# Rotary embedding on one core: three TensorE rows of eight instead of four, and the last tile stored as one transfer

## The chip, the cores and the metric

One core of a Trainium2 chip (trn2). The metric is device time in microseconds; smaller is better. A run's profile also gives its span, the time from the first to the last instruction of the core, which is 1.7 to 2.4 us shorter than the device time. The first three runs of the kernel before agree within 0.05 us (its profiled run took 163.37 us).

## The reference

`x` is 16 batches of 512 positions with 1024 float32 values, seen as 16 heads of 64. Each head is rotated by a per-position table:

```python
x1, x2 = x[..., :32], x[..., 32:]              # halves of each head
cos, sin = cos[None, :, None, :], sin[None, :, None, :]
rotated = concatenate([x1 * cos - x2 * sin, x1 * sin + x2 * cos], axis=-1)
```

So an output is `x * cos + swapped(x) * signed_sin`: two multiplies and an add per element, 33.6 MB in and 33.6 MB out.

## The kernel before

There are eight tiles of 128 partitions. A tile is 4 MiB: per partition eight rows (`k` = 0 to 7) of 1024 values. Loads and stores are all issued from SyncE (SP), in one queue; five tile buffers are allotted in SBUF, the core's working memory, so the loads of tiles 5 to 7 wait for the stores of tiles 0 to 2.

```python
PE_ROWS = (0, 2, 4, 6)       # rows whose sum is made by TensorE in PSUM
DVE_B = ((0,), (0, 4))       # rows whose sine product VectorE makes itself (even, odd tiles)
FIRST = (3, 8)               # tile 0 is loaded as rows 0-2 and rows 3-7
LAST_OUT = (4, 8)            # tile 7 is stored as rows 0-3 and rows 4-7
...
pe = ctx.enter_context(tc.tile_pool(name="pe", bufs=2, space=bass.MemoryType.PSUM))
pd = ctx.enter_context(tc.tile_pool(name="pd", bufs=1, space=bass.MemoryType.PSUM))
...
def add():
    r, ps, b = pending.pop(0)
    nc.vector.tensor_tensor(out=r, in0=ps, in1=b, op=ALU.add)

for t in range(NT):
    xt = tiles[t]
    for k in range(KK):
        r = xt[:, k * dim : (k + 1) * dim]
        own = k in DVE_B[t % 2]
        if not own:
            b = bp.tile([P, dim], FP32, name="b")
            ...
            nc.gpsimd.tensor_tensor(out=halves(b), in0=swapped(r, nh), in1=over_heads(sk), op=ALU.mult)
        if k in PE_ROWS:
            ps = pe.tile([P, dim], FP32, name="ps")
            nc.vector.tensor_tensor(out=pairs(ps), in0=pairs(r), in1=cos_b(k), op=ALU.mult)
            if own:
                nc.vector.tensor_tensor(out=halves(r), in0=halves(r), in1=swapped_signed(k), op=ALU.mult)
            for c in range(0, dim, BANK):
                ...
                nc.tensor.matmul(out=ps[:, c : c + BANK], lhsT=ident, rhs=rhs, start=False, stop=True, ...)
            nc.scalar.copy(out=r, in_=ps)
            while pending:
                add()
        else:
            while pending:
                add()
            ps = pd.tile([P, dim], FP32, name="pd")
            nc.vector.tensor_tensor(out=pairs(ps), in0=pairs(r), in1=cos_b(k), op=ALU.mult)
            pending.append((r, ps, b))
    while pending:
        add()
    if t < NT - 1:
        store(t)
    else:
        lo = 0
        for hi in LAST_OUT:
            store(t, lo, hi)
            lo = hi
    if t + 1 == NT - BUFS:
        for n in range(BUFS, NT):
            load(n)
```

(Cuts are marked with `...`; the code shown is otherwise as in the kernel.) A row costs VectorE one cosine multiply. A TensorE row then gets its sine product added in PSUM, the memory that takes TensorE's sums, by a matmul with the identity, and ScalarE copies the sum back over `x`. Any other row gets a VectorE add. GpSimd makes most sine products.

Of the kernel before, what the change touches and what calls it, by code (L numbers as in the profile page):

```python
# [14 lines left out]
B_BUFS = 6  # L15
BANK = 512

PE_ROWS = (0, 2, 4, 6)

DVE_B = ((0,), (0, 4))  # L20

FIRST = (3, 8)
LAST_OUT = (4, 8)

SIN_PARTS = (64,)
COS_PARTS = (64,)


@with_exitstack
def kernel(  # L30
# [13 lines left out]
    nc = tc.nc  # L44
# [12 lines left out]
    cos_v = cos.rearrange("(p k) j -> p (k j)", k=KK)  # L57
    sin_v = sin.rearrange("(p k) j -> p (k j)", k=KK)
# [18 lines left out]
    def store(t, lo=0, hi=KK):  # L77
        s = slice(lo * dim, hi * dim)
        nc.sync.dma_start(out=out_v[t][:, s], in_=tiles[t][:, s])

    load(0, 0, FIRST[0])
    sin_sb = bp.tile([P, dim], FP32, name="b")[:PB, : KK * half]
    cos_sb = bp.tile([P, dim], FP32, name="b")[:PB, : KK * half]
    for sb, v, parts in ((sin_sb, sin_v, SIN_PARTS), (cos_sb, cos_v, COS_PARTS)):
        lo = 0
        for hi in parts:
            nc.sync.dma_start(out=sb[lo:hi, :], in_=v[lo:hi, :])
            lo = hi
    for lo, hi in zip(FIRST, FIRST[1:]):
        load(0, lo, hi)  # L90
    for t in range(1, BUFS):
# [22 lines left out]
    nc.vector.tensor_copy(out=sns[:, :, 1, :], in_=sin_k)  # L114
    on_dve = sorted(set(DVE_B[0]) | set(DVE_B[1]))
    sns_t = tab[:, KK * half : KK * half + len(on_dve) * hd]
# [7 lines left out]
    def over_heads(s):  # L124
        return bass.AP(tensor=s.tensor, offset=s.offset, ap=[s.ap[0], [0, nh], [1, hd]])

    def swapped(r, n):
        return bass.AP(
            tensor=r.tensor, offset=r.offset + half, ap=[r.ap[0], [hd, n], [-half, 2], [1, half]]
        )  # L130
# [12 lines left out]
    def halves(r):  # L143
        return r.rearrange("p (h a j) -> p h a j", a=2, j=half)
# [7 lines left out]
# [7 lines that stand above are left out]
                sk = sns[:, k].rearrange("p a j -> p (a j)")  # L159
# [3 lines that stand above are left out]
# [3 lines left out]
                for c in range(0, dim, BANK):  # L166
                    rhs = swapped(r[:, c : c + BANK], BANK // hd) if own else b[:, c : c + BANK]
                    nc.tensor.matmul(  # L168
                        out=ps[:, c : c + BANK], lhsT=ident, rhs=rhs, start=False, stop=True, skip_group_check=True
# [14 lines left out]
# [5 lines that stand above are left out]
# [38 lines left out]
```

## Time and profile before

| | before |
|---|---|
| time, median of three runs | 163.11 us |
| span of the profiled run | 161.6 us |
| DMA queue, share of 16 engines' span | 97.5% |
| VectorE busy, last instruction ends | 128.9 us, 142.96 us |
| last store issued, landed | 143.03 us, 160.5 us |
| granted TensorE clock, mean (share of full speed) | 0.833 |

The first lines to read are the page's busy times, its slices (each digit is the busy share of a fortieth of the span, in tenths) and its table of DMA queues (packets, MB, share of the span of all 16 engines).

```profile
PE 81.8 (51%) x136; PEld 30.3 (19%) x136; DVE 128.9 (80%) x115; ACT 33.7 (21%) x33; POOL 121.0 (75%) x58
...
DVE  1059897999999989999999999999999999930000
...
PEclk9999996559975998799969965999689879995555
DMA  5999999999999999999999999999999999999992
...
q1 hardware_dynamic: 2752, 67.24, 97.5%
```

The DMA row has nines from the second slice to the last but one: the queue never runs out of work. VectorE stops four slices earlier. Its 80% looks high, but it has time to spare at the end.

The groups of the page that the change touches (busy time, mean ns of one instruction, idle time before it and what ended that):

```profile
L171 ACT COPY xt<-ps 128x1024 f32<-128x1024 f32 x32 | 32.4, 1012 | 95.2 <-PE ps L168 90.8
L168 PE MATMUL ps<-b,ident 128*128 128x512 f32 x80 | 43.5, 674 | 14.7 <-DVE ps L163 12.1
L150 DVE TENSOR_TENSOR xt<-pd,b 128x1024 f32<-128x1024 f32 x32 | 39.0, 1218 | 2.2 <-POOL b L160 1.1
```

The end of the timeline (start, duration, engine and line; in brackets the idle time before) shows the last row of the last tile. After it, in a separate view of SyncE's timeline, comes the last store.

```profile
139.39 1.96 PE L168 MATMUL ps<-b,ident 128*128 128x512 f32 x4 [1.57 <-DVE ps L163]
...
140.40 1.23 DVE L178 TENSOR_TENSOR pd<-xt,tab 128x1024 f32<-128x1024 f32 x1
141.43 1.01 ACT L171 COPY xt<-ps 128x1024 f32<-128x1024 f32 x1 [2.56 <-PE ps L168]
141.74 1.22 DVE L150 TENSOR_TENSOR xt<-pd,b 128x1024 f32<-128x1024 f32 x1
```

```profile
143.03 0.33 SPq L79 DMA_DIRECT2D out_dram<-xt  x1
```

Three times matter: the matmuls of the last TensorE row take 1.96 us, ScalarE's copy is done at 142.44, and VectorE's last add at 142.96. The store goes out 0.07 us after that.

The DMA view, asked for that one issue, says how long it took to land (KB, us from issue to landing):

```profile
out_dram<-xt SPq DMA_DIRECT2D x1, 2048.0 KB, 17.5
```

A 2 MiB store takes 17.5 us only because it stands behind others. The stretch table (length, then busy time and instruction count of PE, PEld, DVE, ACT and POOL, then granted clock, DMA share and GB/s) shows that the engines are fed throughout:

```profile
148.00:149.00 1.00, 0.00 (x0) 0.00 (x0) 0.00 (x0) 0.00 (x0) 0.00 (x0) 0.50 0.61 262
149.00:150.00 1.00, 0.00 (x0) 0.00 (x0) 0.00 (x0) 0.00 (x0) 0.00 (x0) 0.50 0.88 377
150.00:152.00 2.00, 0.00 (x0) 0.00 (x0) 0.00 (x0) 0.00 (x0) 0.00 (x0) 0.50 1.03 442
152.00:154.00 2.00, 0.00 (x0) 0.00 (x0) 0.00 (x0) 0.00 (x0) 0.00 (x0) 0.50 1.05 451
```

A caution on the page's chain of waits: here it ends with VectorE's last add at 142.96 and says "DVE 37%". It does not contain the 18.6 us of stores that follow. The bound of this kernel has to be read from the DMA row.

### The profile page before, as it was taken

To read this page: it belongs to the slowest core of one execution; us is meant where nothing else is said; L and a number is where in the kernel's file an instruction comes from. 1 tells how busy PE (TensorE), PEld (TensorE's weight loads), DVE (VectorE), ACT (ScalarE), POOL (GpSimd) and SP (SyncE) were. 2 spreads that over 40 slices of the span, in tenths; PEclk is the share of its full clock that TensorE was granted. 3 is DMA by queue.
4 is the path that set the end of the run, shared out by engine and by line. 5 is a ranking of instruction groups with operands and counts; after the bars stand their busy time and mean duration, and the time that the engine had idled before them with its cause. 6 is when DMAs were issued, how large, how long until landed. Compare 5 with 4: busy or idle time off the path is not lost.

```text
span 161.6 us, 692 instructions
## 1 busy us (share of the span) xinstructions
PE 81.8 (51%) x136; PEld 30.3 (19%) x136; DVE 128.9 (80%) x115; ACT 33.7 (21%) x33; POOL 121.0 (75%) x58
## 2 busy tenths in 40 slices
PE   4136946496429742955097419660984194600000
PEld 1112301241114211311032114210321131100000
DVE  1059897999999989999999999999999999930000
ACT  0003242023302430223113302222223122220000
POOL 1049999999999999999994199999999997000000
PEclk9999996559975998799969965999689879995555
DMA  5999999999999999999999999999999999999992
GB/s 189 395 441 435 454 454 389 446 462 389 438 470 389 389 446 464 389 454 446 397 454 446 397 448 446 406 454 438 406 450 438 406 448 438 414 454 389 438 426 118
DMA packets 2756, 67.28 MB, mean 416 GB/s; under 512 B 320, under 2 KB 448, under 8 KB 448
## 3 DMA queue, kind: packets, MB, share of 16 engines
q1 hardware_dynamic: 2752, 67.24, 97.5%
q8 instruction: 1, 0.02, 0.0%
q14 instruction: 3, 0.02, 0.0%
HBM read 33.69 MB, written 33.55 MB: 416 GB/s over the span
## 4 chain that ended last, share of the span: by engine, by line
DVE 37%; PE 18%; issue 17%; POOL 6%; ACT 4%; DMA 4%; SPq 0%; DVEq 0%; ACTq 0%; POOLq 0%
PE ps L168 17%; DVE xt L150 12%; DVE pd L178 12%; DVE ps L163 7%; POOL b L160 6%; DVE xt L165 5%; ACT xt L171 4%; DMA b<-in_sin_dram 4%; PE tab L110 1%; PE tab L111 1%; DVE tab L118 0%; DVE sns L113 0%; SPq L75 0%; DVE sns L114 0%; DVEq L150 0%
## 5 line engine op out<-in xcount | busy, mean ns | idle before, releaser
L160 POOL TENSOR_TENSOR b<-xt,sns 128x1024 f32<-128x1024 f32 x52 | 120.3, 2350 | 14.5 <-DVE sns L114 9.2
L168 PE MATMUL ps<-xt,ident 128*128 128x512 f32 x48 | 35.8, 888 | 39.2 <-issue 24.5
L171 ACT COPY xt<-ps 128x1024 f32<-128x1024 f32 x32 | 32.4, 1012 | 95.2 <-PE ps L168 90.8
L168 PE MATMUL ps<-b,ident 128*128 128x512 f32 x80 | 43.5, 674 | 14.7 <-DVE ps L163 12.1
L150 DVE TENSOR_TENSOR xt<-pd,b 128x1024 f32<-128x1024 f32 x32 | 39.0, 1218 | 2.2 <-POOL b L160 1.1
L163 DVE TENSOR_TENSOR ps<-xt,tab 128x1024 f32<-128x1024 f32 x32 | 39.1, 1223 | 1.5 <-ACT xt L171 1.3
L178 DVE TENSOR_TENSOR pd<-xt,tab 128x1024 f32<-128x1024 f32 x32 | 39.3, 1227 | 0.8
L168 PEld LDWEIGHTS ps<-b,ident 128*128 128x128 f32 x80 | 17.1, 227 | 44.1 <-issue 30.6
L168 PEld LDWEIGHTS ps<-xt,ident 128*128 128x128 f32 x48 | 11.6, 267 | 58.8 <-issue 46.1
L165 DVE TENSOR_TENSOR xt<-xt,tab 128x1024 f32<-128x1024 f32 x12 | 14.6, 1220 | 0.4
L113 DVE TENSOR_SCALAR sns<-tab 128x256 f32<-128x256 f32 x1 | 0.4, 425 | 8.0 <-PE tab L111 8.0
L171 ACT ACT_TABLE_LOAD x1 | 1.3, 1283 | 13.5 <-DVE xt L165 13.5
L110 PE MATMUL tab<-b,spread 64*128 64x256 f32 x2 | 1.2, 697 | 4.5 <-DMA b<-in_sin_dram 4.5
L101 PE MATMUL ps<-zero 128*128 128x512 bf16 x4 | 1.9, 625 | 1.2 <-DVE zero L97 1.2
L110 PEld LDWEIGHTS tab<-b,spread 64*128 64x128 f32 x2 | 0.5, 308 | 5.4 <-issue 5.4
L111 PE MATMUL tab<-b,spread 64*128 64x256 f32 x2 | 1.1, 631 | 0.0
L97 DVE MEMSET zero<- 128x256 uint32 x1 | 0.3, 272 | 0.9 <-PEq L208 0.9
L101 PEld LDWEIGHTS <-zero 128*128 128x128 bf16 x4 | 0.4, 129 | 1.7 <-DVE zero L97 1.2
L111 PEld LDWEIGHTS tab<-b,spread 64*128 64x128 f32 x2 | 0.7, 333 | 0.2
L118 DVE COPY tab<-sns 128x64 f32<-128x64 f32 x2 | 0.5, 228 | 0.1
L109 DVE COPY spread<-ident 64x64 f32<-64x64 f32 x2 | 0.3, 182 | 0.2 <-POOL ident masks.py:199 0.2
masks.py:197 POOL MEMSET ident<- 128x128 f32 x1 | 0.2, 204 | 0.3 <-POOLq L208 0.3
(6 smaller groups left out, 1.1 us busy)
## 6 DMA issues: line engine op xcount, KB each, us to landing
xt<-in_x_dram SPq DMA_DIRECT2D x7, 4096.0 KB, 29.5
out_dram<-xt SPq DMA_DIRECT2D x7, 4096.0 KB, 30.3
out_dram<-xt SPq DMA_DIRECT2D x2, 2048.0 KB, 18.1
xt<-in_x_dram SPq DMA_DIRECT2D x1, 2560.0 KB, 11.3
xt<-in_x_dram SPq DMA_DIRECT2D x1, 1536.0 KB, 6.2
b<-in_sin_dram SPq DMA_DIRECT2D x1, 64.0 KB, 6.3
b<-in_cos_dram SPq DMA_DIRECT2D x1, 64.0 KB, 6.1
```

Of the source, the lines that this page charges most:

```text
L101: nc.tensor.matmul(out=ps[:, c : c + BANK], lhsT=zero[:, :P], rhs=zero, start=True, stop=True)
L110: nc.tensor.matmul(out=sin_t, lhsT=spread, rhs=sin_sb, start=True, stop=True)
L111: nc.tensor.matmul(out=cos_t, lhsT=spread, rhs=cos_sb, start=True, stop=True)
L113: nc.vector.tensor_scalar_mul(out=sns[:, :, 0, :], in0=sin_k, scalar1=-1.0)
L118: nc.vector.tensor_copy(out=sns_t[:, i * hd : (i + 1) * hd], in_=sns[:, k])
L150: nc.vector.tensor_tensor(out=r, in0=ps, in1=b, op=ALU.add)
L160: nc.gpsimd.tensor_tensor(out=halves(b), in0=swapped(r, nh), in1=over_heads(sk), op=ALU.mult)
L163: nc.vector.tensor_tensor(out=pairs(ps), in0=pairs(r), in1=cos_b(k), op=ALU.mult)
L165: nc.vector.tensor_tensor(out=halves(r), in0=halves(r), in1=swapped_signed(k), op=ALU.mult)
L168: nc.tensor.matmul(out=ps[:, c : c + BANK], lhsT=ident, rhs=rhs, start=False, stop=True, skip_group_check=True)
L171: nc.scalar.copy(out=r, in_=ps)
L178: nc.vector.tensor_tensor(out=pairs(ps), in0=pairs(r), in1=cos_b(k), op=ALU.mult)
```

## The change

The intent: give one TensorE row in four back to VectorE, which then pairs its product and its add in its own PSUM buffer, and send the last tile as one transfer. (The PSUM pools were already separate, `pe` and `pd`; only the assignment of rows changes. The rows whose sine product VectorE makes itself have to be TensorE rows, so the second one of odd tiles moves from 4 to 3. `SIN_PARTS` and `COS_PARTS` held one part each, so those lines change nothing.)

```diff
-PE_ROWS = (0, 2, 4, 6)
+PE_ROWS = (0, 3, 6)
-DVE_B = ((0,), (0, 4))
+DVE_B = ((0,), (0, 3))
 FIRST = (3, 8)
-LAST_OUT = (4, 8)
-SIN_PARTS = (64,)
-COS_PARTS = (64,)
+LAST_OUT = (8,)
...
-    for sb, v, parts in ((sin_sb, sin_v, SIN_PARTS), (cos_sb, cos_v, COS_PARTS)):
-        lo = 0
-        for hi in parts:
-            nc.sync.dma_start(out=sb[lo:hi, :], in_=v[lo:hi, :])
-            lo = hi
+    nc.sync.dma_start(out=sin_sb, in_=sin_v)
+    nc.sync.dma_start(out=cos_sb, in_=cos_v)
```

## The prediction

> **What bounds the kernel now.** The DMA queue. The queue table puts the main queue at 97.5% of 16 engines' span (67.2 MB, mean 416 GB/s over 161.6 us), and the stretch table shows about 430 GB/s in every 10 us from 10 to 150. VectorE is next: 128.9 us busy, and in the timeline almost gapless from 10.96 to 142.96 us. After that only stores drain: the last one is issued at 143.0 and lands at 160.5 (17.5 us to landing, although it carries 2.1 MB, 4.9 us at 428 GB/s). So VectorE has slack against the queue. The tile-6 store (issued 126.25, landing 150.85) keeps the engines fed until about 149.2; the two half stores of tile 7 follow without a gap. At the end the engines stop moving data at about 159.0, landing follows 1.5 us later, the span ends 1.1 us after that.
>
> **What the change moves.** Per tile one row goes from TensorE/ScalarE (accumulate, 1.01 us copy) to VectorE (one more add, 1.22 us). Eight adds in all; ScalarE loses 8 copies, TensorE 16 matmuls, GpSimd stays at 52 multiplies, bytes stay the same. From start-to-start distances in the timeline (1.13 to 1.14 us after an unrelated instruction, 1.25 to 1.26 where a buffer is reused, 1.33 where an add reads the product just before it) I rebuild the new VectorE order: 17.07 us for an even tile and 18.34 for an odd one (the same sum for the old order gives 15.43 and 16.70; the timeline has 15.4 to 16.2 and 16.8 to 17.1). Tile 0 does not get longer: its last add waits for GpSimd's seventh product (26.74) in both. VectorE should then end at about 152.5 us instead of 142.96. GpSimd, at 2.31 us per row, stays ahead and its loads arrive at unchanged times, so I expect no new waits.
>
> **How much is on the critical path.** Up to tile 6 nothing: its store is issued at about 134 instead of 126, the queue holds work until 149.2. Then it matters that tile 7 goes out as one transfer: it can only be issued when VectorE has finished, at 152.6, so the queue runs dry. First data came 0.9 us after the first issue of the kernel (0.73 to 1.6), so engines idle from 149.2 to about 153.5. 4.19 MB at 428 GB/s are 9.8 us: data ends at 163.3, landing 164.8, span 165.9. That is 4.3 us more. The Trainium skill ("DMA: Bandwidth & Descriptors", section on where the 2 us go) says most of a transfer's fixed cost is the write receipt after the last byte; the trace agrees with 1.5 us at the end. Each half alone should be nearly free: with two halves, the first would be issued near 145 and bridge the gap; with the old rows, VectorE is done at 143.
>
> **Predicted time: 167.3 us, range 166.3 to 168.5.** Chances: faster by over 2% 0.01, within 2% 0.17, slower by over 2% 0.82.
>
> **What the profile would show.** Right: VectorE busy near 138.6 us and ending near 152.5; last store issued at about 152.6 and landing 12 us later; a dip to zero in DMA between 149 and 153.5 and nowhere else; ScalarE with 24 copies, about 24 us; TensorE less busy. Wrong: DMA gaps earlier, VectorE waits for GpSimd or ScalarE beyond the present few tenths, or a last landing under 11 us.
>
> **What would make it wrong.** VectorE ending before 150 (then the queue never runs dry and the time is 163); stores moving faster through an otherwise empty queue; later stores delaying loads 5 to 7, so that GpSimd stalls (slower than 168).

## The result, and the profile after

The changed kernel took 167.96 us (median of six runs, 167.07 to 168.68) against 163.13 us (six runs, 163.08 to 163.17): ratio 1.0293, 95% interval 1.0261 to 1.0326. Ratios here are the mean time of one kernel's runs over that of the other's runs of the same rounds, so not quite the ratio of the medians. Note the spread: 1.6 us after, 0.1 us before.

The page of the changed kernel, the same parts as above:

```profile
PE 86.7 (52%) x104; PEld 27.1 (16%) x104; DVE 139.6 (84%) x123; ACT 25.6 (15%) x25; POOL 121.4 (73%) x58
...
DVE  1069999999999999999999999999999999998000
...
PEclk9999985595855585555675558555555555586555
DMA  5999989999899998989999899999999999980885
...
q1 hardware_dynamic: 2608, 67.24, 95.0%
...
L162 PE MATMUL ps<-b,ident 128*128 128x512 f32 x48 | 40.0, 980 | 26.6 <-DVE ps L157 16.2
L144 DVE TENSOR_TENSOR xt<-pd,b 128x1024 f32<-128x1024 f32 x40 | 48.8, 1221 | 2.5
...
L165 ACT COPY xt<-ps 128x1024 f32<-128x1024 f32 x24 | 24.3, 1013 | 114.3 <-PE ps L162 109.4
```

There is one zero in the DMA row, right before the last store. Bytes are unchanged. TensorE does 32 instructions less and is busy 4.9 us *longer*: the clock row is mostly fives, and a matmul of the same shape takes 980 ns instead of 674.

The end of the timeline after:

```profile
149.32 3.09 PE L162 MATMUL ps<-b,ident 128*128 128x512 f32 x4 [2.49 <-DVE ps L157]
...
150.34 1.23 DVE L172 TENSOR_TENSOR pd<-xt,tab 128x1024 f32<-128x1024 f32 x1
...
151.67 1.22 DVE L144 TENSOR_TENSOR xt<-pd,b 128x1024 f32<-128x1024 f32 x1
152.50 1.01 ACT L165 COPY xt<-ps 128x1024 f32<-128x1024 f32 x1 [4.61 <-PE ps L162]
153.53 0.33 SPq L76 DMA_DIRECT2D out_dram<-xt  x1
```

VectorE ends at 152.89, close to the predicted 152.5. But the store does not follow it: it follows ScalarE's copy of row 6 (ends at 153.51), because that row's four matmuls took 3.09 us instead of 1.96. SyncE's waits (us in total, times, longest) have six for ScalarE's copies; in the kernel before they have none:

```profile
SPq L76 <- ACT xt L165: 5.9, 6, 1.3
```

The DMA view of that last store, then the stretch table:

```profile
out_dram<-xt SPq DMA_DIRECT2D x1, 4096.0 KB, 11.1
```

```profile
148.00:149.00 1.00, 0.00 (x0) 0.00 (x0) 1.00 (x2) 0.00 (x0) 0.00 (x0) 1.00 0.23 98
149.00:150.00 1.00, 0.68 (x2) 0.47 (x3) 1.00 (x2) 0.00 (x0) 0.00 (x0) 1.00 0.00 0
150.00:152.00 2.00, 2.00 (x3) 0.35 (x2) 1.86 (x3) 0.00 (x0) 0.00 (x0) 0.50 0.00 0
152.00:154.00 2.00, 0.42 (x1) 0.00 (x0) 0.89 (x1) 1.01 (x1) 0.00 (x0) 0.50 0.00 0
154.00:156.00 2.00, 0.00 (x0) 0.00 (x0) 0.00 (x0) 0.00 (x0) 0.00 (x0) 0.50 1.23 524
```

The queue runs dry where before it had two half stores to work on. How long is it dry? A finer stretch table of the same kernel shows a trap in reading this:

```profile
148.25:148.50 0.25, 0.00 (x0) 0.00 (x0) 0.25 (x1) 0.00 (x0) 0.00 (x0) 1.00 0.91 393
154.25:154.50 0.25, 0.00 (x0) 0.00 (x0) 0.00 (x0) 0.00 (x0) 0.00 (x0) 0.50 4.56 1966
154.75:155.00 0.25, 0.00 (x0) 0.00 (x0) 0.00 (x0) 0.00 (x0) 0.00 (x0) 0.50 0.00 0
155.50:155.75 0.25, 0.00 (x0) 0.00 (x0) 0.00 (x0) 0.00 (x0) 0.00 (x0) 0.50 4.99 2097
```

A share of 4.99 in a quarter of a microsecond is 1.25 us on each of the 16 engines: the table books a whole packet in the slice where it begins (it cannot be where it ends, as 154.25 is only 0.72 us after the issue and a packet lasts 1.22). So the last packets of the tile-6 store, booked at 148.25 to 148.50, are still at work after that. Asked in finer steps, the trace has the last of them begin before 148.33, so it ends at about 149.5 (that store landed at 149.95: issued at 135.85, 14.1 us to landing), and the first packet of the last store begins at 154.37. The queue is dry from about 149.5 to 154.4, some 4.8 us. The span grew by 4.1 us (161.6 to 165.7). The queue's busy time is the same in both (97.5% of 161.6 and 95.0% of 165.7 are 157.6 and 157.4 us), so all of that growth is idle time of the queue; the kernel before has some idle time of its own.

### The profile page after: what moved, and what is told of

Read it like the earlier page. It is cut to its first block, busy times and chain, and to the rows that moved or that the text cites. A ratio compares the mean times of both kernels' runs of the same rounds, so it can differ in the third digit from the quotient of the medians.

```text
span 165.7 us, 609 instructions
## 1 busy us (share of the span) xinstructions
PE 86.7 (52%) x104; PEld 27.1 (16%) x104; DVE 139.6 (84%) x123; ACT 25.6 (15%) x25; POOL 121.4 (73%) x58
## 4 chain that ended last, share of the span: by engine, by line
DVE 71%; issue 13%; DMA 4%; PE 3%; ACT 1%; DVEq 0%; SPq 0%; ACTq 0%
DVE pd L172 29%; DVE xt L144 23%; DVE ps L157 10%; DVE xt L159 9%; DMA b<-in_sin_dram 4%; PE ps L162 2%; PE tab L104 1%; ACT xt L165 1%; PE tab L105 1%; DVEq L144 0%; DVE tab L112 0%; DVE sns L107 0%; SPq L72 0%; DVE sns L108 0%; DVEq L159 0%
## 5 line engine op out<-in xcount | busy, mean ns | idle before, releaser
L162 PE MATMUL ps<-xt,ident 128*128 128x512 f32 x48 | 42.8, 1044 | 33.3 <-issue 18.8
L162 PE MATMUL ps<-b,ident 128*128 128x512 f32 x48 | 40.0, 980 | 26.6 <-DVE ps L157 16.2
L144 DVE TENSOR_TENSOR xt<-pd,b 128x1024 f32<-128x1024 f32 x40 | 48.8, 1221 | 2.5
L172 DVE TENSOR_TENSOR pd<-xt,tab 128x1024 f32<-128x1024 f32 x40 | 49.1, 1228 | 1.1
L165 ACT COPY xt<-ps 128x1024 f32<-128x1024 f32 x24 | 24.3, 1013 | 114.3 <-PE ps L162 109.4
L157 DVE TENSOR_TENSOR ps<-xt,tab 128x1024 f32<-128x1024 f32 x24 | 29.3, 1222 | 0.0
L162 PEld LDWEIGHTS ps<-xt,ident 128*128 128x128 f32 x48 | 13.2, 303 | 61.9 <-issue 57.1
L162 PEld LDWEIGHTS ps<-b,ident 128*128 128x128 f32 x48 | 12.2, 282 | 54.5 <-POOL b L154 29.6
```

## The experiments

My theory T: the extra VectorE work is free while the queue is full, and the single last store is free while VectorE ends early; together, the last store is issued after the queue has run dry, and every microsecond of lateness is paid. Rival A: the added VectorE instructions or their memory traffic slow the kernel as such. Rival B: one large last store costs by itself. A second question is why the changed kernel spreads by 1.6 us: the ScalarE and TensorE ending, or the DMA side.

All diffs are against the changed kernel unless said otherwise; all results were correct.

| run | ratio to before (95% interval) | median us (lowest to highest) | last store issued (profiled run) | span |
|---|---|---|---|---|
| rows only | 1.0014 (0.9998 to 1.0029) | 163.57 (163.06 to 163.74) | 148.11 and 154.28 | 161.6 |
| store only | 0.9984 (0.9970 to 0.9998) | 163.02 (162.82 to 163.19) | 142.70 | 161.2 |
| fewer own | 0.9977 (0.9963 to 0.9991) | 162.89 (162.61 to 163.13) | 148.72 | 160.9 |
| row 5 | 1.0248 (1.0233 to 1.0264) | 167.29 (167.15 to 167.51) | 153.02 | 165.2 |
| changed again | 1.0299 (1.0273 to 1.0324) | 168.28 (167.37 to 168.63) | 154.07 | 166.2 |
| more own | 1.0618 (1.0602 to 1.0634) | 173.26 (173.06 to 173.66) | 159.29 | 171.4 |
| split after row 6 | 1.0084 (1.0063 to 1.0105) | 164.43 (164.33 to 165.19) | 150.11 and 153.93 | 162.4 |
| keep warm | 1.0229 (1.0212 to 1.0246) | 167.10 (166.55 to 167.20) | 153.20 | 165.3 |
| tables from ScalarE | 1.0192 (1.0172 to 1.0213) | 166.33 (165.90 to 166.89) | 152.75 | 164.8 |
| fewer own, halves | 0.9988 (0.9973 to 1.0003) | 163.06 (162.67 to 163.46) | 142.57 and 148.81 | 160.9 |

The kernel before had medians of 163.21, 163.20 and 163.22 us beside the three groups of runs (the first four, the next four, the last two).

### Rows only

```diff
-LAST_OUT = (8,)
+LAST_OUT = (4, 8)
```

> Three matmul rows as in the changed kernel, but the last tile goes out as two halves as before. My theory (the queue runs dry because one whole-tile store has to wait for the last instruction of the tile): the first half is issued when row 3 is copied, near 148, so the queue is nearly continuous; 163.1 to 164.0 us, ratio to before 1.000 to 1.006, although VectorE still ends near 152.9. Rival A (the extra VectorE adds or their memory traffic cost the time themselves): nearly the changed kernel's time, 167 to 168 us.

Measured 163.57 us, ratio 1.0014, within the expectation of T. VectorE was busy 139.6 us here too and its last instruction ended at 152.98, as in the changed kernel. Rival A falls: 10 us more VectorE work costs nothing that is clear of zero. The first half was issued at 148.11, just before the tile-6 store was finished, and bridged the gap; only a short one is left at 154.5 to 155.1, before the second half:

```profile
148.00:150.00 2.00, 0.59 (x1) 0.50 (x2) 2.00 (x3) 0.08 (x1) 0.00 (x0) 0.50 0.73 311
150.00:152.00 2.00, 2.00 (x3) 0.67 (x2) 1.86 (x3) 0.00 (x0) 0.00 (x0) 0.50 0.95 401
152.00:154.00 2.00, 1.16 (x2) 0.00 (x0) 0.98 (x1) 0.76 (x1) 0.00 (x0) 0.50 0.94 401
```

### Store only

Against the kernel before:

```diff
-LAST_OUT = (4, 8)
+LAST_OUT = (8,)
```

> The four matmul rows of the kernel before, with only the last store made one transfer. My theory: the store is issued at about 143, some 6 us before the queue would run dry, so no gap: 163.0 to 163.5 us, ratio 0.998 to 1.003. Rival B (one large last store costs by itself): 165 us or more.

Measured 163.02 us, ratio 0.9984. Rival B falls too: the single store, issued at 142.70 into a queue that is still full, costs nothing; if anything it gains 0.2%. So neither part alone costs, and the cost is in their combination.

### Fewer own products on VectorE

```diff
-DVE_B = ((0,), (0, 3))
+DVE_B = ((0,), (0,))
```

> The changed kernel, with the second sine product of each odd tile given from VectorE back to GpSimd (4 products of 1.22 us off VectorE, 4 of 2.35 us onto GpSimd). My theory: VectorE ends about 4.7 us earlier, near 148, the last copy at 148.5 to 149, so the gap in the DMA queue shrinks from 5.5 us to about 1: 163.0 to 164.3 us. Rival A (uniform slowing by VectorE's added traffic): only a part of 4.7 us comes back and DMA never stands still or stands still as long; about 166 us. If GpSimd became the limit it would be slower than 165.

Measured 162.89 us, just under the range: the whole loss is gone, with three TensorE rows and one last store. VectorE ended at 147.78, the store was issued at 148.72, while the tile-6 store was still at work. GpSimd, with four more products, did not become the limit.

```profile
148.00:149.00 1.00, 0.00 (x0) 0.00 (x0) 0.00 (x0) 0.70 (x1) 0.00 (x0) 1.00 0.23 98
149.00:150.00 1.00, 0.00 (x0) 0.00 (x0) 0.00 (x0) 0.00 (x0) 0.00 (x0) 1.00 1.22 524
```

Packets begin again in the stretch 149 to 150, where the changed kernel has 0.00. This variant also beats both given kernels, by 0.23% over the kernel before; that is small.

### More own products on VectorE

```diff
-DVE_B = ((0,), (0, 3))
+DVE_B = ((0, 3), (0, 3))
```

> The changed kernel with a second VectorE sine product in even tiles too: 4 more VectorE instructions, 4 fewer on GpSimd. My theory: VectorE ends 5.1 us later (4 times 1.27), near 158.0, the DMA queue runs dry at 148.5 as before, and the whole 5.1 us is added to the changed kernel's time: 172.3 to 173.8 us. If the loss were a fixed cost of the single store, it would stay near 168.

Measured 173.26 us, ratio 1.0618. The last store was issued at 159.29, 5.2 us later than in the second set of runs of the changed kernel (154.07), and its span was 5.2 us longer (171.4 against 166.2). Together with the run before, this is the dose and the response. The queue did not run dry at 148.5 as expected: it was dry from 139.9 to 141.8, before the tile-6 store (issued at 140.93), and again from 151.7 to 160.1; the end follows the last issue all the same. In all seven runs with a whole last tile issued at or after 148.72, the span is the time of that issue plus 12.1 or 12.2 us:

| run | issue | span | difference |
|---|---|---|---|
| fewer own | 148.72 | 160.9 | 12.2 |
| tables from ScalarE | 152.75 | 164.8 | 12.1 |
| row 5 | 153.02 | 165.2 | 12.2 |
| keep warm | 153.20 | 165.3 | 12.1 |
| changed (first profile) | 153.53 | 165.7 | 12.2 |
| changed again | 154.07 | 166.2 | 12.1 |
| more own | 159.29 | 171.4 | 12.1 |

In the store-only run the difference is 18.5: there the queue, not the issue, sets the end. An estimate of the latest issue that costs nothing is 161.2 less 12.1, about 149.1; "fewer own" is just before it.

### Split after row 6

```diff
-LAST_OUT = (8,)
+LAST_OUT = (6, 8)
```

> The changed kernel with the last store cut after row 6 of 8 (three quarters, then one quarter). My theory: the first piece is issued when row 5 is added, about 150.4, so the queue stands still for only about 2.5 us (148.5 to 151) instead of 5.5, and the second piece is queued behind it before it ends: about 165.1 us (164.5 to 165.8), between the rows-only variant (163.6) and the changed kernel (168). If only a cut in halves mattered, or a cut at all, it would equal one of the two.

Measured 164.43 us, between the two as expected, but 0.1 us under the range. The median missed because I had read the end of the tile-6 store 1.2 us too early, in the way shown above; the first piece was issued at 150.11, just as the last packet of the tile-6 store ended, and the queue stood still for 0.9 us (150.06 to 150.94), not 2.5.

### Row 5 instead of row 6

```diff
-PE_ROWS = (0, 3, 6)
+PE_ROWS = (0, 3, 5)
```

> The changed kernel with the third matmul row moved from row 6 to row 5: the same number of instructions on every engine, but the last ScalarE copy is done well before VectorE's last add. In the changed kernel's trace the last store waited for that copy (ends 153.51) and not for VectorE (152.89), because four slow matmuls took 3.09 us. If this ScalarE and TensorE ending also makes the run-to-run spread (167.07 to 168.68), then the time falls to about 167.3 and the spread is under 0.5 us; if the spread comes from the DMA side, it stays 1.5 us.

Measured 167.29 us, 167.15 to 167.51. Instruction counts and VectorE's end (152.96) are those of the changed kernel, but ScalarE's last copy ended at 151.07, and the store followed VectorE (issued 153.02). The time fell to what was expected, and the spread with it.

### The changed kernel again

> The changed kernel unaltered, on the same chip as the next three runs: 167 to 168.7 us with a spread of over 1 us, as in its first six runs. It is the yardstick for the spread of the third variant here.

Measured 168.28 us, 167.37 to 168.63. In this profile the last matmuls took 3.75 us, the copy ended at 154.04, and the store went out at 154.07, although VectorE was done at 152.77.

### Keep TensorE warm

```diff
+    warm = pfix.tile([P, BANK], FP32)
...
         nc.vector.tensor_tensor(out=r, in0=ps, in1=b, op=ALU.add)
+        nc.tensor.matmul(out=warm, lhsT=ident, rhs=r[:, :BANK], start=True, stop=True)
```

> The changed kernel with one idle 128x512 f32 matmul into a spare PSUM bank after every VectorE add, only to keep TensorE busy between its rows; the result is not used. If TensorE's longer pauses (about 2.4 us every 6) are what lowers its granted clock from 0.83 to 0.63 to 0.70 and makes the last row's matmuls take 3.1 to 3.75 us instead of 1.96, then the clock rises to over 0.8, the last copy ends before VectorE's last add, the last store is issued near 152.9, and the time is 167.2 us with a spread under 0.5 us. If the pauses do not set the clock, the clock stays low, and the time is 168 us or more.

Measured 167.10 us, 166.55 to 167.20. *Adding* 80 matmul instructions made the kernel 1.2 us faster than the changed one on the same chip (168.28), with the clock at 0.90 to 0.92 instead of 0.66 to 0.70. The end of its timeline:

```profile
149.56 1.95 PE L165 MATMUL ps<-b,ident 128*128 128x512 f32 x4 [1.36 <-DVE ps L160]
...
151.60 1.01 ACT L168 COPY xt<-ps 128x1024 f32<-128x1024 f32 x1 [5.16 <-PE ps L165]
151.91 1.23 DVE L146 TENSOR_TENSOR xt<-pd,b 128x1024 f32<-128x1024 f32 x1
...
153.20 0.33 SPq L76 DMA_DIRECT2D out_dram<-xt  x1
```

The row's matmuls are back at 1.95 us, the copy ends before VectorE's last add, and the store follows VectorE. The spread, 0.65 us, was half that of the changed kernel (1.26), not under 0.5 as expected. So the pauses of TensorE lowered its clock, and through the last copy the clock cost some 1 us of the changed kernel's time. The row-5 run, with that copy off the end, spread by only 0.36 us (four runs, another chip), so the copy probably makes most of the spread too; what makes the 0.65 us here is not shown.

### Two tries at a faster version

The first, against the "fewer own" variant:

```diff
-    nc.sync.dma_start(out=sin_sb, in_=sin_v)
-    nc.sync.dma_start(out=cos_sb, in_=cos_v)
+    nc.scalar.dma_start(out=sin_sb, in_=sin_v)
+    nc.scalar.dma_start(out=cos_sb, in_=cos_v)
```

> A try at a version that beats both: three matmul rows, the second sine product of odd tiles on GpSimd (the variant that measured 162.89), and the two small table loads issued from ScalarE's queue, so that the x loads follow each other on SyncE without the 1.1 us that issuing the tables takes there. If the gap in DMA data near 2 to 2.8 us comes from the issue order, up to 0.6 us is gained: 162.3 to 162.7 us. If the first load alone keeps the engines fed, nothing changes: 162.6 to 163.1 us.

Measured 166.33 us: neither branch of the expectation, and a loss clear of noise (1.0172 to 1.0213, on both sides of 2%). The cosine table landed at 12.2 us (issued at 1.30, 10.9 us to landing) instead of 8.0 in the "fewer own" run (1.73 and 6.3), so VectorE's main work began at 14.58 us instead of 10.91, the last store went out at 152.75 instead of 148.72, and the span grew by 3.9 us. The waits view of this run gives TensorE's wait for the table (us in total, times, longest):

```profile
PE tab L105 <- DMA b<-in_cos_dram: 3.0, 1, 3.0
```

I had taken the table loads for a cost of SyncE's issue time and forgotten that they stand before most of the x loads there; that this order is why the cosine table came later is likely, but not tested. As a test of T it is a welcome accident: VectorE's lateness came from the start of the kernel this time, and the end paid for it by the same rule.

The second, against the "fewer own" variant again, is `LAST_OUT = (4, 8)`.

> The same three-row variant with the last tile stored in halves, tables on SyncE. The data of the first half can then be queued from about 143, so no wait is left at the end and the time is set by the bytes: 162.6 to 163.1 us, within 0.2% of the whole-tile version, as in that version the gap was already under 1 us. If the last whole-tile store still cost something there, this is faster by 0.5 us or more.

Measured 163.06 us, 0.9988 of before, with an interval that touches 1: as expected, nothing is left to gain at the end once VectorE is in time. The whole-tile version (0.9977) remains the fastest measured; the two intervals overlap.

## Why the prediction was right

The forecast was 167.3 us (166.3 to 168.5) and slower by over 2%; measured were 167.96 and, in the second set, 168.28 us. Point by point:

- *What bounds the kernel*: right. Rows only and store only, both free, show that up to the last store neither VectorE nor TensorE sets the time.
- *VectorE's end*: predicted 152.5, measured 152.89 and 152.77. Adding up start-to-start distances from the trace (1.13 unrelated, 1.25 on a reused buffer, 1.33 on a product just made) was good to 0.4 us over 140. Busy time was 139.6 instead of 138.6.
- *No new waits, GpSimd ahead*: right for VectorE and GpSimd; GpSimd waited for VectorE, never the reverse. Wrong for the stores: SyncE's six waits for ScalarE are new.
- *Only the combination costs*: right, by three experiments and by the rule "issue plus 12.1".
- *When the store goes out*: predicted 152.6, measured 153.53 and 154.07. The step that failed is "VectorE should then end at about 152.5 us ... it can only be issued when VectorE has finished". The tile is finished by two engines, and I did not cost the other: ScalarE's copy of row 6, behind matmuls that I took to be as fast as before. "TensorE less busy" was wrong in sign (86.7 us against 81.8). The keep-warm run shows the cause: with rows three apart TensorE pauses longer and runs at a lower clock.
- *The dry time and the landing*: predicted dry from 149.2 to 153.5, then 9.8 us of data and 1.5 us to landing. Measured: dry from about 149.5 to 154.4, data to about 164.3 by estimate (the last packet begins before 163.08 and one lasts 1.2 us), landing at 164.6. The 1.5 us "after the data" was a misreading of the booking of packets; most of it was the last packet itself, which the predicted sum (0.9 to the first data, 9.8 of data, 1.5 to landing) so counts twice. Issue to landing came out at 11.1 us against the predicted 12.2. By luck, this error of 1.1 us made up for the later issue (0.9 us), which is why the predicted span (165.9) is so near the measured ones (165.7 and 166.2).

One thing stays open: the tile-6 store landed 0.9 us sooner in the changed kernel's profile (149.95 against 150.85) although it was issued 9.6 us later. The cause is not known; it gains nothing there, as the queue then waits.

## What to carry to other kernels

When a queue is kept full, lateness upstream is free up to the moment when the queue would run empty, and paid in full after it; so find that moment in the trace and compare the issue of the last transfer with it. Cutting the last transfer in two buys slack exactly there: here it was worth the 4 us that the added VectorE work would otherwise cost. And before giving an engine less work, check whether its pauses grow: TensorE with a quarter fewer matmuls was slower in each, and on the last row that counted.

## What the Trainium skill lacked or had wrong

- "TensorE: Matmul & The Clock Gate", section "Why this matters for your kernels", advises no idle gaps over about 3 us between bursts of matmuls. Here shorter ones were enough. In the changed kernel's profile no pause after 107.8 us is longer than the bracketed 2.49, and yet the clock is 0.50 up to 146.5, and again from 150.0 after only 3.4 us at full speed; the rows there take 3.09 to 3.75 us. A low clock also hides long pauses: most rows start some 6.1 us apart, and the only row at full speed (1.95 us, at 18.57) is followed by a pause of 4.16. In the kernel before, pauses of about 1.6 us (the bracketed 1.57) went with 1.96 us for a row of four. That idling lowers the clock agrees with the page, and the keep-warm run (0.91) shows it; the limit here was lower.
- "DMA: Bandwidth & Descriptors", section "Anatomy of one DMA", gives 2.0 us plus bytes over 436 GB/s for transfers issued from GpSimd, and puts most of the 2 us after the last byte. An estimate from that formula for 4.19 MB is 11.6 us; the last store, issued from SyncE into an empty queue, took 11.1. The split differs: the first packet begins 0.84 us after the issue, and landing is about 0.4 us after the estimated end of the last packet. The page gives no such split for transfers issued from SyncE.
- "VectorE: DVE Perf Modes", section "The DRAIN you can't avoid", reports that a semaphore after each of a chain of copies costs nothing extra. It gives no figure for what dependence costs, and here it was not nothing: starts were 1.13 us apart for unrelated instructions and 1.33 us where an add reads the product just before it (150.34 to 151.67 above). With 1.13 throughout, an even tile's 14 instructions would take 15.8 us by estimate; the trace of the changed kernel has 17.08 for tile 2 (46.52 to 63.60).
- No page says that this profile's stretch table books a DMA packet whole where it begins (shares of 4.99 in a 0.25 us slice).
